# Splitting the closing of a mixer step in a DeltaNet + RWKV-7 decoder block: branch A's norm, gate and store traced behind branch B's projections

## The chip, the cores and the metric

The kernel runs on one core of one Trainium2 chip. The time is device time in microseconds, from one launch to its end. The engines are named as the profile names them: PE is TensorE (PEld its weight loads), DVE is VectorE, ACT is ScalarE, POOL is GpSimd, SP is the sync engine, which here issues most DMAs.

## The reference, cut to what matters

One decoder block in float32 on 1024 tokens of width 1024, with 16 learned tokens ahead of them: half a SwiGLU, then two mixers side by side on the same normed input, merged and projected, then another half SwiGLU.

```python
u = _rmsnorm(h, mix_norm[l])
aq, ak, av, az, abeta, aalpha, bcols, ga, gb = jnp.split(u @ w_in[l], ...)
o_a = _deltanet_branch(aq, ak, av, az, abeta, aalpha, ...)   # A: 8 heads of 128
o_b = _rwkv7_branch(bcols, ...)                              # B: 16 heads of 64
merged = jax.nn.sigmoid(ga) * o_a + jax.nn.sigmoid(gb) * o_b
h = h + merged @ w_out[l]
...
# the end of A (what `finish_a` computes), o from the chunked scan:
o = o * lax.rsqrt(jnp.mean(o * o, axis=-1, keepdims=True) + EPS) * out_gain
o = o.reshape(bsz, t, A_WV) * jax.nn.silu(z)
# the end of B (what stays in `finish`), y from the scan:
y = (y - mean) * lax.rsqrt(var + B_GN_EPS) * ln_gain + ln_bias
y = y + jnp.sum(r * k * r_k, axis=-1, keepdims=True) * v
return y.reshape(bsz, t, B_W) * gate
```

## The kernel before

Activations lie transposed: 128 channels on the partitions, tokens along the free axis. The two SwiGLU halves (`ffn1`, `ffn2`) stand at the two ends; `middle` holds the mixers, from about 700 to 2260 us of the span.

**Steps.** The mixers run in 16 steps: two segments of tokens (528 tokens with the learned ones, then 512), and in each eight groups `j` of 128 channels, one head of A and two heads of B. Steps 0 to 7 are the first segment, 8 to 15 the second. In the text a step n is counted from its `bq` matmuls, the last of its chain (step 10: 1826.0 to 1913.7 us). Each step consists of actions:

- `decay`: B's decay factors (`pw`, `pa` on PE, `sw`, `av` on ACT, the scan `Ls` on DVE).
- `new_b`: B's three projections v, k, r (each `pp`, 24 products of 512 columns in the second segment, 48 of 272 or 256 in the first), the token shift, the key norm (column sum `cs<-hl,bdr`), and the bonus: `bv` is made on DVE, split on ACT and DVE into a high and a low part `hl`, summed over channels on PE (`bon`), and multiplied by v on DVE.
- `new_a`: A's projections k, q, v, its short convolution (`acc` on DVE), SiLU (`xr` on ACT), and the norms of k and q (`cs<-hl,onesr`).
- `operands`, `inverses`: the chunks' triangular matrices and their inversion. `inverses` is 31 pairs `tb`, `Xb` on DVE, each depending on the one before.
- `merge_blocks`, `transitions`, `chains`: the merge of the inverses (`iv`), the transition products (`xp`, `mp`, `np`) and the serial scan over chunks (`p`, `b`, `pq`, closed by `bq`).
- `gates`: three projections (z and the two merge gates) and `gat`.
- `finish`: the closing. For A: squares of the scan's output `oa` (it lies in the tile `kq`), split in two parts `hl`, their sum over channels by two PE products with a matrix of ones (`cs<-hl,onesr`), rsqrt as Ln and Exp (`ro`), two DVE products. For B the same with a block matrix (`cs<-hl,bdr`, `rg`), and four DVE operations on `yb`. Then `yb += oa` and one DMA of `yb` (128x512 float32) to the buffer `mdr`.

**What sets the order.** The program text is traced in the order of strings (`REGULAR` and four others for special steps), where `x+` means action `x` of the next step and `x++` of the step after that. A list scheduler turns this into one fixed order per engine at compile time: among what it takes to be ready it prefers what was traced first. Every engine then executes its own list strictly in that order, and waits on semaphores. DMAs issued by SP stand in one list too.

**Shared tiles.** `ro`, `rg` and one tile of `gates` share one buffer (tag `ro`). The pair `hl` of a column sum is one buffer: its next user waits until the products of the last one are done. `kq`, `Va`, `yb` exist twice, `zg` and `gg` once. A projection's split weights `w` exist twice: ACT makes the high part (line 162), DVE the low part (line 163).

## Time and profile before

| | us |
|---|---|
| time before, median of 3 runs (lowest, highest) | 2966.39 (2959.74, 2974.48) |
| the profiled execution: time, span | 2963.86, 2961.3 |
| PE busy in the span | 2847.0 (96%) |
| DVE busy | 2209.8 (75%) |
| ACT busy | 1445.5 (49%) |
| POOL busy | 522.5 (18%) |
| 40 slices | PE 9 tenths or more in nearly all, PEclk 9 in all |

How to read it: PE bounds the kernel nearly everywhere, so a change can only gain PE's idle time, or time in which PE's clock is not granted in full. The share of a stage is what counts, and in the mixers DVE is nearly as busy as PE. In a timeline row the columns are start in us, length in us, engine, line, operation, out<-in, shapes and count; the bracket at its end is the idle time of the engine ahead of it and what released it. Rows of one line that follow each other are merged.

### The profile page before, as it was taken

The page shows a single profiled execution, that of the slowest core. Times are in us where ns is not written, and L with a number is a line of the kernel's source. Part 1 is how long each engine was busy: PE and PEld are TensorE (multiplying, and loading weights), DVE is VectorE, ACT ScalarE, POOL GpSimd, SP SyncE. Part 2 cuts the span into 40 slices and gives each one's busy share as a digit, 9 for nine tenths or more (in the row PEclk, how much of TensorE's full clock was granted, in tenths as well). Part 3 has the DMA queues.
Part 4 walks back from the last instruction along what each step waited for, and adds up shares of the span by engine and source line. Part 5 has one row for each costly group of instructions (what it writes and reads, how often), then busy time and mean ns, then how long its engine had stood idle before and what let it go on. Part 6 is the DMA issues. An engine that isn't in the chain of part 4 may idle for free. (4 is left out here: it accounts for less than half of the span.)

```text
span 2961.3 us, 60777 instructions
## 1 busy us (share of the span) xinstructions
PE 2847.0 (96%) x24552; PEld 2472.5 (83%) x24552; DVE 2209.8 (75%) x4119; ACT 1445.5 (49%) x2511; POOL 522.5 (18%) x630
## 2 busy tenths in 40 slices
PE   8999999999989999999998999999999999999998
PEld 8999999999878887888776777777777888888887
DVE  8666668776677887788867887778876866667886
ACT  6322234336555656556566556556644432223443
POOL 0332232323000000011001010111101032332521
PEclk9999999999999999999999999999999999999999
DMA  5333236553222322323332332233354332223763
GB/s 213 126 108 108 95 120 215 174 192 125 67 75 75 87 66 73 84 76 86 97 88 74 82 84 72 75 87 83 105 143 175 129 113 102 97 98 129 258 215 109
DMA packets 287897, 339.17 MB, mean 115 GB/s; under 512 B 172704, under 2 KB 181024, under 8 KB 287616
## 3 DMA queue, kind: packets, MB, share of 16 engines
q1 hardware_dynamic: 283600, 326.10, 35.3%
q0 software_dynamic: 2000, 6.56, 0.6%
q8 instruction: 193, 3.16, 0.4%
q10 hardware_dynamic: 2016, 2.63, 0.3%
q14 instruction: 88, 0.72, 0.1%
HBM read 267.57 MB, written 73.41 MB: 115 GB/s over the span
## 5 line engine op out<-in xcount | busy, mean ns | idle before, releaser
L314 PE MATMUL pp<-uk,w 128*128 128x512 f32 (+2 forms) x4824 | 978.6, 348 | 16.8 <-DVE w L163 9.1
L314 PEld LDWEIGHTS pp<-uk,w 128*128 128x128 f32 x4824 | 749.2, 191 | 111.5 <-DVE w L163 12.6
L741 PE MATMUL pd<-form,w 128*128 128x256 f32 (+2 forms) x2904 | 438.0, 313 | 4.7 <-DVE w L163 4.7
L741 PEld LDWEIGHTS pd<-form,w 128*128 128x128 f32 x2904 | 404.3, 190 | 38.1 <-DVE w L163 5.9
L520 PE MATMUL pg<-bt,w 128*128 128x256 f32 (+2 forms) x2520 | 401.6, 318 | 2.5 <-DVE w L163 2.5
L520 PEld LDWEIGHTS pg<-bt,w 128*128 128x128 f32 x2520 | 360.3, 188 | 36.4 <-DVE w L163 3.7
L526 DVE TENSOR_TENSOR c<-c,pg 128x520 f32<-128x520 f32 (+1 forms) x280 | 189.6, 689 | 243.6 <-PE pg L520 220.4
L163 DVE TENSOR_TENSOR w<-wraw,w 128x1024 fp32r<-128x1024 f32 (+1 forms) x254 | 336.5, 1325 | 37.5 <-ACT w L162 36.0
L520 PE MATMUL pg<-b,w 128*128 128x256 f32 (+2 forms) x2160 | 348.1, 317 | 0.0
L162 ACT ACTIVATE w<-wraw 128x1024 fp32r<-128x1024 f32 (+1 forms) x254 | 267.3, 1053 | 160.9 <-PE pg L520 117.1
L520 PEld LDWEIGHTS pg<-b,w 128*128 128x128 f32 x2160 | 309.8, 188 | 28.3 <-DVE w L163 0.2
L162 ACT ACTIVATE w<-wrx 128x1024 fp32r<-128x1024 f32 (+1 forms) x64 | 58.4, 912 | 277.8 <-PE pg L520 241.8
L490 POOL TENSOR_TENSOR wrx<-wrx 128x512 f32<-128x512 f32 x38 | 52.5, 1380 | 611.9 <-DVE w22b L163 352.6
L163 DVE TENSOR_TENSOR form<-form 128x520 fp32r<-128x520 f32 (+1 forms) x152 | 145.3, 991 | 12.4 <-ACT form L162 11.8
L162 ACT ACTIVATE w<-wsum 128x768 fp32r<-128x768 f32 x96 | 75.7, 789 | 158.6 <-PE pd L741 127.2
L163 DVE TENSOR_TENSOR w<-wsum,w 128x768 fp32r<-128x768 f32 x96 | 114.2, 1195 | 37.1 <-ACT w L162 37.0
L241 POOL TENSOR_TENSOR wsum<-wsum,wraw 128x768 f32<-128x768 f32 (+1 forms) x48 | 96.4, 2022 | 205.0 <-DMA wraw<-in_wdn 196.9
L1705 DVE TENSOR_TENSOR Xb<-Xb,tb 115x126 f32<-115x126 f32 (+22 forms) x496 | 125.4, 253 | 8.2
L162 ACT ACTIVATE form<-form 128x520 fp32r<-128x520 f32 (+1 forms) x152 | 93.8, 632 | 76.3 <-DMA form<-frm 72.0
L1703 DVE TENSOR_TENSOR tb<-Ub,Xb 115x126 f32<-115x126 f32 (+22 forms) x496 | 125.1, 252 | 8.0
L1513 DVE SCALAR_TENSOR_TENSOR acc<-xr,pk,acc 128x528 f32<-128x528 f32 (+1 forms) x144 | 109.1, 758 | 24.1 <-ACT acc L1509 23.4
L314 PE MATMUL pwo<-uk,w 128*128 128x512 f32 x384 | 94.7, 397 | 2.7 <-DVE ho L1180 1.5
(445 smaller groups left out, 4360.8 us busy)
## 6 DMA issues: line engine op xcount, KB each, us to landing
wraw<-in_win SPq DMA_DIRECT2D x150, 512.0 KB
wraw<-in_wgu SPq DMA_DIRECT2D x44, 512.0 KB
wrx<-in_wgu SPq DMA_DIRECT2D x44, 512.0 KB
frm<-c SPq DMA_DIRECT2D x76, 260.0 KB
form<-frm SPq DMA_DIRECT2D x76, 260.0 KB
frm<-c SPq DMA_DIRECT2D x76, 256.0 KB
form<-frm SPq DMA_DIRECT2D x76, 256.0 KB
wraw<-in_wdn SPq DMA_DIRECT2D x34, 384.0 KB
```

Of the source, the lines that this page charges most:

```text
L162: g.nc.scalar.activation(hi, src, AF.Copy)
L163: (eng or g.nc.vector).tensor_tensor(lo, src, hi.bitcast(F32), op=ALU.subtract)
L241: g.nc.gpsimd.tensor_tensor(s, x, y, op=ALU.add if r == 1 else ALU.subtract)
L314: g.last_product = g.nc.tensor.matmul(ps, lhsT=l, rhs=r, start=i == 0, stop=i == n - 1)
L490: sums.tensor_tensor(a22, a21, a22, op=ALU.add)
L520: nc.tensor.matmul(ps[:, c0 : c0 + cn], lhsT=l[:, x, k, :], rhs=r[:, k, y, c0 : c0 + cn], start=i == 0, stop=i == 3 * HK - 1)
L526: nc.vector.tensor_tensor(o, x, y, op=ALU.add)
L741: nc.tensor.matmul(pd[:, c0 : c0 + cn], lhsT=wd[:, u, k - k0, :], rhs=x[:, v, c0 : c0 + cn], start=k + i == 0, stop=k == HF - 1 and i == 2)
L1513: nc.vector.scalar_tensor_tensor(acc[:, :n], xr[:, tap : tap + n], V("convw", ct * 4 + tap), acc[:, :n], op0=ALU.mult, op1=ALU.add)
L1703: nc.vector.tensor_tensor(tv, U[:, i, i + 1 :].unsqueeze(2).to_broadcast([npt, nt, ncc]), X[:, i, 0:ncc].unsqueeze(1).to_broadcast([npt, n ...
L1705: nc.vector.tensor_tensor(X[:, i + 1 :, 0:ncc], X[:, i + 1 :, 0:ncc], tv, op=ALU.add)
```

## The change

`finish` is cut in two. B's half keeps the name and the place. A's half, with the sum of both and the store, becomes `finish_a`. In the regular steps and in the switch step it is traced behind `new_b` of two steps ahead and in front of `new_a`; in the three other orders it follows `finish` directly. No operation is added or removed; the only other difference inside a closing is that B's operations now come ahead of A's.

```diff
-REGULAR = "merge_blocks transitions operands+ inverses+ chains gates finish decay++ new_b++ new_a++"
-BEFORE_SWITCH = "... chains gates finish banks gates+ segment decay++ new_b++ tokens++ new_a++"
-SWITCH = "merge_blocks transitions operands+ inverses+ chains finish decay++ new_b++ new_a++"
-LAST_BUT_ONE = "merge_blocks transitions operands+ inverses+ chains gates finish"
-FINAL = "gates merge_blocks transitions chains finish fill"
+REGULAR = "merge_blocks transitions operands+ inverses+ chains gates finish decay++ new_b++ finish_a new_a++"
+BEFORE_SWITCH = "... chains gates finish finish_a banks gates+ segment decay++ new_b++ tokens++ new_a++"
+SWITCH = "merge_blocks transitions operands+ inverses+ chains finish decay++ new_b++ finish_a new_a++"
+LAST_BUT_ONE = "merge_blocks transitions operands+ inverses+ chains gates finish finish_a"
+FINAL = "gates merge_blocks transitions chains finish finish_a fill"
...
 def finish(g, q):
     nc, st, V, j = g.nc, g.st, g.V, q.j
-    oa, yb, zg, gg = q.oa, q.yb, q.zg, q.gg
-    sq = q.Va.rearrange("p c m -> p (c m)")
-    ro = st.tile([P, FULL], F32, name="ro", tag="ro")
-    colsum_rsqrt(g, "ones", oa, sq, ro, FULL, 1.0 / P, V("eps"), pool="ch")
-    nc.vector.tensor_tensor(oa, oa, ro, op=ALU.mult)
-    nc.vector.scalar_tensor_tensor(oa, oa, V("aog"), zg, op0=ALU.mult, op1=ALU.mult)
+    yb = q.yb
     sq = q.AR[:, :NCB].rearrange("p c m -> p (c m)")
     ...
-    nc.vector.tensor_tensor(yb, yb, gg, op=ALU.mult)
+    nc.vector.tensor_tensor(yb, yb, q.gg, op=ALU.mult)
+
+
+def finish_a(g, q):
+    nc, st, V, j = g.nc, g.st, g.V, q.j
+    oa, yb = q.oa, q.yb
+    sq = q.Va.rearrange("p c m -> p (c m)")
+    ro = st.tile([P, FULL], F32, name="ro", tag="ro")
+    colsum_rsqrt(g, "ones", oa, sq, ro, FULL, 1.0 / P, V("eps"), pool="ch")
+    nc.vector.tensor_tensor(oa, oa, ro, op=ALU.mult)
+    nc.vector.scalar_tensor_tensor(oa, oa, V("aog"), q.zg, op0=ALU.mult, op1=ALU.mult)
     nc.vector.tensor_tensor(yb, yb, oa, op=ALU.add)
     if q.it + 1 < 2 * NJ:
         nc.sync.dma_start(g.mdr[q.s][j], yb)
```

What this does to the engines' lists is seen best in step 10. PE behind the chain's last products; before, A's column sum (`cs<-hl,onesr`) stands between the two `pw`:

```order
L1956 MATMUL gat<-gds,ug 128x512 x2
L1956 MATMUL gat<-g_18051,ug 128x512
L1412 MATMUL pw<-ws,upz 128x512
L1292 MATMUL cs<-hl,onesr 128x512 x2
L1413 MATMUL pw<-ws,upz 128x512
L1416 MATMUL pa<-as,upz 128x512
L1417 MATMUL pa<-as,upz 128x512
L314 MATMUL pp<-uk,w 128x512 x5
L1292 MATMUL cs<-hl,bdr 128x512
L314 MATMUL pp<-uk,w 128x512 x2
L1292 MATMUL cs<-hl,bdr 128x512
```

The same place of the same engine in the changed kernel, and then further down, behind the bonus sum `bon`, where A's two products now stand:

```order
L1956 MATMUL gat<-gds,ug 128x512 x3
L1956 MATMUL gat<-g_18051,ug 128x512
L1412 MATMUL pw<-ws,upz 128x512
L1413 MATMUL pw<-ws,upz 128x512
L1416 MATMUL pa<-as,upz 128x512
L1417 MATMUL pa<-as,upz 128x512
L314 MATMUL pp<-uk,w 128x512 x7
L1292 MATMUL cs<-hl,bdr 128x512
L314 MATMUL pp<-uk,w 128x512 x2
L1292 MATMUL cs<-hl,bdr 128x512
L314 MATMUL pp<-uk,w 128x512 x39
```

```order
L314 MATMUL pp<-uk,w 128x512 x37
L1292 MATMUL bon<-hl,bdr 128x512
L314 MATMUL pp<-uk,w 128x512 x7
L1292 MATMUL bon<-hl,bdr 128x512
L314 MATMUL pp<-uk,w 128x512 x4
L1292 MATMUL cs<-hl,onesr 128x512
L314 MATMUL pp<-uk,w 128x512 x2
L1292 MATMUL cs<-hl,onesr 128x512
L314 MATMUL pp<-uk,w 128x512 x22
```

A's sum moved from in front of `new_b`'s 72 products to behind them and `bon`; B's sum now has seven projection products ahead of it instead of five. The list of DVE at the same place, before (`yb<-bq,yb` is the sum that B's closing starts from, `hl<-Va,hl` the low part of A's squares, `hl<-AR,hl` that of B's):

```order
L1307 TENSOR_TENSOR hl<-Va,hl 128x512
L1703 TENSOR_TENSOR tb<-Ub,Xb 115x120
L1705 TENSOR_TENSOR Xb<-Xb,tb 115x20x6
L1927 TENSOR_TENSOR yb<-bq,yb 128x512
L1703 TENSOR_TENSOR tb<-Ub,Xb 115x133
L163 TENSOR_TENSOR w<-wraw,w 128x1024
L1705 TENSOR_TENSOR Xb<-Xb,tb 115x19x7
L1957 TENSOR_TENSOR gg<-gat,gg 128x512
L1703 TENSOR_TENSOR tb<-Ub,Xb 115x126
L1307 TENSOR_TENSOR hl<-AR,hl 128x512
```

And now:

```order
L1703 TENSOR_TENSOR tb<-Ub,Xb 115x133
L163 TENSOR_TENSOR w<-wraw,w 128x1024
L1705 TENSOR_TENSOR Xb<-Xb,tb 115x19x7
L1927 TENSOR_TENSOR yb<-bq,yb 128x512
L1703 TENSOR_TENSOR tb<-Ub,Xb 115x126
L1957 TENSOR_TENSOR gg<-gat,gg 128x512
L1705 TENSOR_TENSOR Xb<-Xb,tb 115x18x7
L163 TENSOR_TENSOR ug<-ugr,ug 128x128
L1703 TENSOR_TENSOR tb<-Ub,Xb 115x136
L1941 TENSOR_TENSOR ug<-ugr,ug 32x128
L1705 TENSOR_TENSOR Xb<-Xb,tb 115x17x8
L1307 TENSOR_TENSOR hl<-AR,hl 128x512
```

A's operation is gone, and `yb<-bq,yb` went from in front of the weight split `w<-wraw,w` to behind it. In the list of DMAs the store `mdr<-yb` moved from ahead of the inverses' traffic to behind it, between two weight loads and the small load `gp`.

## The prediction

> **What bounds the kernel now.** I read the table of engines and the slices first (PE 96% of the span), then the waits of PE in the mixers, then one step in order of time. The windows give the size of what can be won:

> ```profile
> 870.00:2260.00 1390.00, 1321.65 (x14269) 1084.08 (x14267) 1094.74 (x2626) 824.92 (x1579) 118.14 (x309) 0.99 0.31 86
> ...
> 1826.00:1913.70 87.70, 83.05 (x873) 66.36 (x872) 70.51 (x167) 52.50 (x99) 9.22 (x18) 0.98 0.30 81
> 1913.70:1999.80 86.10, 81.45 (x873) 65.12 (x872) 70.44 (x167) 52.54 (x99) 9.23 (x18) 1.00 0.30 83
> ```

> The columns are the stretch, its length, and the busy time of PE, PEld, DVE, ACT and POOL, then the granted clock. From 870 to 2260 us, sixteen steps, PE idles 1390 - 1322 = 68 us. No matmul is added or taken away, so the change can win at most these 68 us, and what a halved clock costs on top. The two step rows are steps 10 and 11: the same work, 1.6 us apart, with a clock of 0.98 and 1.00. Who ends PE's waits in the same stretch:

> ```profile
> PE bon L1292 <- ACT hl L162: 12.2, 13, 1.9
> PE cs L1292 <- ACT hl L1306: 11.8, 19, 1.1
> PE np L1356 <- DVE AR L1842: 9.1, 14, 1.2
> PE pp L314 <- DVE w L163: 5.2, 7, 2.8
> PE cs L1292 <- ACT vka L1805: 5.1, 8, 0.9
> ...
> PE cs L1292 <- DVE yb L1927: 1.5, 1, 1.5
> ```

> Two of these are A's closing itself: `cs` on `vka` and on `yb`, 6.6 us, are A's column sum standing in front of `pw` (row 1829.12 below). The `cs` on `hl` are B's closing and the norms in `new_a`. The first row, the bonus sum, is none of the closing's instructions, but hangs on it, as step 10 shows on PE:

> ```profile
> 1827.86 0.40 PE L1412 MATMUL pw<-ws,upz 128*128 128x512 f32 x1
> 1829.12 0.70 PE L1292 MATMUL cs<-hl,onesr 128*128 128x512 f32 x2 [0.86 <-ACT vka L1805]
> ...
> 1831.50 0.39 PE L1292 MATMUL cs<-hl,bdr 128*128 128x512 f32 x1
> ...
> 1832.18 0.40 PE L1292 MATMUL cs<-hl,bdr 128*128 128x512 f32 x1
> ...
> 1848.46 8.57 PE L314 MATMUL pp<-uk,w 128*128 128x512 f32 x37
> 1858.92 0.50 PE L1292 MATMUL bon<-hl,bdr 128*128 128x512 f32 x1 [1.89 <-ACT hl L162]
> 1859.26 2.84 PE L314 MATMUL pp<-uk,w 128*128 128x512 f32 x7
> ```

> and on DVE, one window and some rows of step 10:

> ```profile
> 1826.90:1861.00 34.10, 31.35 (x176) 24.99 (x169) 33.19 (x77) 22.36 (x39) 7.79 (x14) 0.98 0.41 104
> ...
> 1827.13 0.69 DVE L1307 TENSOR_TENSOR hl<-Va,hl 128x512 fp32r<-128x512 f32 x1
> 1827.74 0.32 DVE L1703 TENSOR_TENSOR tb<-Ub,Xb 115x120 f32<-115x120 f32 x1
> 1828.29 0.69 DVE L1927 TENSOR_TENSOR yb<-bq,yb 128x512 f32<-128x512 f32 x1
> 1829.09 1.22 DVE L163 TENSOR_TENSOR w<-wraw,w 128x1024 fp32r<-128x1024 f32 x1
> 1832.03 0.69 DVE L1967 TENSOR_TENSOR kq<-kq,ro 128x512 f32<-128x512 f32 x1
> 1832.85 0.75 DVE L1968 SCALAR_TENSOR_TENSOR kq<-kq,pk,zg 128x512 f32<-128x512 f32 x1
> 1837.25 0.68 DVE L1975 TENSOR_TENSOR yb<-yb,kq 128x512 f32<-128x512 f32 x1
> 1857.46 0.74 DVE L1485 SCALAR_TENSOR_TENSOR bv<-rB,pk,kB 128x512 f32<-128x512 f32 x1
> ```

> DVE is busy for 33.2 of the 34.1 us from the closing to `bon`. So `bv`, which `bon` waits for, comes when DVE has worked off its list, and every microsecond of A's closing in that list stands ahead of it. That is the main lever of the change, more than A's own wait.

> **The change part by part.** A step's half A is, on PE, two column products; on ACT the square into `Va` (which keeps its place), the square into `hl`, Ln and Exp of `ro`; on DVE the four rows above, `hl<-Va,hl`, two on `kq`, and the last sum on `yb`; on SP one store. All of them move except that one square.

> *A's own wait* goes: the chain's `vka` and the weight split held ACT back from A's `hl`, PE stood 0.86 us. Now `pw` follows `gat` at once. 6.6 us less.

> *B's column sum takes over a part of it.* PE now has twelve products of 0.23 us (8.57 / 37) between the same `gat` and B's first sum (one more `gat`, two `pw`, two `pa`, seven `pp`): 1827.86 + 2.8 = 1830.6. B's `hl` is not there yet. On DVE A's `hl` is gone (-0.61, the distance of the rows 1827.13 and 1827.74), but a `tb`, the weight split and an `Xb` come ahead of `yb` (0.3 + 1.2 + 0.2): it starts at 1829.3 to 1829.4 and ends at 1830.1. ACT needs two squares then:

> ```profile
> 1829.46 0.63 ACT L1305 ACTIVATE AR<-yb 128x512 f32<-128x512 f32 x1
> 1829.98 0.68 ACT L1311 ACTIVATE ro<-cs,pk 128x512 f32<-128x512 f32 x1
> 1830.55 0.63 ACT L1306 ACTIVATE hl<-yb 128x512 fp32r<-128x512 f32 x1
> ```

> They start 0.5 us apart, so `hl` is done at about 1831.3, and PE stands 0.7 us. The low part on DVE has six operations between `yb` and itself, 2.0 us, and ends at 1832.65: PE, two `pp` further, stands another 0.65 us. At 1832.9 it has 39 products ahead of it; before, it had 41 at 1832.4. Nothing is won up to here. In the first segment the same count (12 smaller `pp`, `gat`, `pw`, `pa`, 2.8 us behind the chain, against `hl` some 4 us behind it) gives a wait of about 1.25 us, where now stand 0.5 to 1.1:

> ```profile
> 1080.88 0.50 PE L1292 MATMUL cs<-hl,bdr 128*128 128x512 f32 x1 [0.50 <-ACT hl L1306]
> ...
> 1174.31 0.50 PE L1292 MATMUL cs<-hl,bdr 128*128 128x512 f32 x1 [1.14 <-ACT hl L1306]
> ```

> Costs: 1.4 us in four steps 10 to 13, about 0.5 in steps 8 and 9 each, 0.3 in six steps of the first segment: 5.6 + 1 + 2 = 8.6 us. The bounds are 0 (B's part is ready whenever PE comes) and 19 us (1.5 in each of 13 steps).

> *The bonus sum comes earlier.* Four operations leave DVE's list ahead of `bv`. Each delays the next by 0.60 to 0.66 us, 2.5 us together, and the list stays full: k's and r's projections end where they did, and DVE reaches `kB` and `rB` after them. So `bv` comes at about 1855.0 to 1855.5, ACT's split 0.8 later, and PE comes at 1832.9 + 39, 24 and 37 products + two short groups = 1857.2: no wait left. Of the 12.2 us in the list, the switch step's 1.4 stays (below), and up to 0.8 I leave for small ones: 10 us less. Bounds 4 (only what exceeds a shortening by 0.5) and 12.2.

> *The clock.* Behind the wait of step 10 PE took 2.84 us for seven products, 0.41 instead of 0.23 each:

> ```profile
> 1859.70:1863.10 3.40, 3.40 (x9) 2.64 (x8) 2.26 (x4) 0.00 (x0) 1.71 (x3) 0.50 0.44 155
> 2033.70:2037.10 3.40, 3.40 (x9) 2.67 (x9) 2.49 (x5) 0.00 (x0) 1.52 (x3) 0.51 0.50 161
> ...
> 1946.62 0.50 PE L1292 MATMUL bon<-hl,bdr 128*128 128x512 f32 x1 [1.84 <-ACT hl L162]
> ```

> In steps 10 and 12 the clock was granted by half for one stretch of 3.4 us behind `bon`; in step 11, with a wait of 1.84 us there, it was not, and that step's row above has 1.00. That is the 1.6 us between the steps' lengths. Without the wait the halving goes: 2 x 1.6 = 3.2 us less. [...]

> *The switch step 7* has the largest waits, and no gates' products to fill them:

> ```profile
> 1594.94 0.73 PE L314 MATMUL pp<-uk,w 128*128 128x512 f32 x2 [2.11 <-ACT acc L1509]
> 1597.06 0.80 PE L1292 MATMUL bon<-hl,bdr 128*128 128x512 f32 x1 [1.39 <-ACT hl L162]
> ...
> 1601.72 1.65 PE L314 MATMUL pp<-uk,w 128*128 128x512 f32 x3 [2.85 <-DVE w L163]
> ```

> `bon` comes some 2 us earlier by DVE's list, but PE gets there earlier too (`vp` now stands behind `bon`), and A's two products, which wait for `hl` twice, directly behind. I take 2 us less; bounds +2 and -11 (6.4 of waits and half of the halved clock behind them).

> *A's new place* lies between `bon` and the convolutions of `new_a`. Its cover there, in step 10:

> ```profile
> 1863.00:1885.00 22.00, 20.99 (x255) 15.91 (x256) 14.61 (x26) 19.23 (x36) 0.96 (x4) 1.00 0.19 60
> 1863.81 0.60 ACT L1508 ACTIVATE xr<-pp 128x512 f32<-128x512 f32 x1 [4.93 <-PE pp L314]
> ```

> DVE has 7.4 us free and takes 2.5. ACT has 2.8 free behind 1863 and 4.9 ahead of it: A's `hl` falls into the 4.9, Ln and Exp (1.1 us) into the fuller part. Behind them wait SiLU, a weight split and the first norm's sum of `new_a`, which PE waits for already (0.4 us). I take 1 us over all steps; bounds 0 and 1.1 x 13 = 14. PE's two products there are the ones that left the other place.

> *The store* now stands on SP behind two weight loads and ahead of `gp`. `yb` should be done at about 1866.3, `gp` was issued at 1868.25 and is used on DVE from 1876.5 on, and the loads behind it wait for a weight split anyway:

> ```profile
> 1868.25 0.37 SPq L1570 DMA_DIRECT2D gp<-gdr  x1
> ...
> 1876.52 1.14 DVE L1574 SCALAR_TENSOR_TENSOR E<-gp,tk,ck 128x128 f32<-128x128 f32 x4
> ```

> Nothing, with 8 us of cover. If A came that late, `E` and behind it the chain would wait. The buffers (`ro`, `kq`, `zg`) are taken again only a step or a projection later: nothing.

> Sum: -6.6 + 8.6 - 10 - 3.2 - 2 + 1 = -12.2. The profiled execution took 2963.9 (2961.3 of span and 2.6 around it), which gives 2951.7; it lies 2.5 below the median of the runs, 2966.4, and from that I predict 2954.

> **The rivals.**
> *Nothing takes the wait over.* B's squares are ready when PE comes, since ACT has no `ro` between them, and the switch step runs through. Then the 8.6 fall away, and step 7 gives 6 more: -27, 2939. For it: PE's waits in the first segment are short and the list is the scheduler's own; against it: the weight split ahead of `yb`, which is in the list.
> *Given back on ACT.* The 1.1 us delay `new_a` in all 13 steps, 14 us: +1 or so in all, 2966. For it: ACT is at 19.2 of 22 us there, against it DVE's free time and PE's queue of `pp`.
> *Slower: the halved clock moves to B's sum.* It decides from about 1.86 us of idle within 3.4, as in step 10. If B's wait in the first segment is 2.2 instead of 1.25, six steps pay 1.3 more than now and 1.7 of clock, 18 us, and the other steps only exchange their halving. With `bon` in those six won back (2.7) and the rest of the sum near 0 the time is 2981. Against it: a miss of a microsecond in a list worked out to some tenths. That the change does nothing is excluded by the lists, except in steps 6, 14 and 15.

> **How the numbers follow.** About 0.5%, 15 us, is what a measurement of this kernel can tell from no change. My forecast, 2946 to 2962, gets 0.48, and a third of it is below 2951.6; the first rival 0.22, the second 0.17, the third 0.13. Faster: 0.16 + 0.22 + a little = 0.40; same: 0.32 + 0.17 - 0.02 = 0.47; slower 0.13. The range leaves out the outer ends of the first and third: 2934 to 2974.

> **What would show it.** In the new profile: no wait at A's `cs` of more than some tenths; a wait of 1.0 to 1.5 us at B's (two parts); `bon` almost without one from step 8 on; a clock of 1.00 in steps 9 to 13; step 11 at about 84.5 us instead of 86.1; the waits at `np` as now. The prediction is wrong if DVE idles ahead of `bv` (then the list was not what held it), or if the waits in `new_a` exceed 1 us per step.

## The result, and the profile after

The changed kernel takes 2953.3 us (median of 6 runs, 2942.97 to 2955.89), the kernel before beside it 2964.77. The ratio is 0.9947 with an interval of [0.9931, 0.9963] (the quotient of the two medians is 0.9961); the same kernel run once more in a later set gave 0.9969 [0.9958, 0.9981]. So it is faster, by 0.2 to 0.7% if both intervals are taken together. The prediction was 2954.

The profiled execution took 2947.1 (span 2945.0), 16.7 less than the one of before. Not all of this belongs to the change: the first `bq` came 3.6 us earlier, in a stretch that the change leaves alone (in the later execution of the changed kernel it came 4.9 later). From the first `bq` to that of step 15 are 1348.4 us before, 1334.8 after and 1336.2 in the later execution: 12 to 14 us less, against 12.2 in the sum of the prediction. The windows of the two kernels, steps 0 to 5, 6 to 8 and 9 to 13 (columns as in the prediction):

```profile
896.00:1450.80 554.80, 531.27 (x6253) 454.88 (x6253) 437.51 (x1082) 328.06 (x658) 42.69 (x143) 1.00 0.30 81
1450.80:1739.30 288.50, 268.35 (x2678) 211.25 (x2678) 223.85 (x518) 176.01 (x321) 24.55 (x58) 0.96 0.30 79
1739.30:2173.20 433.90, 412.14 (x4345) 328.74 (x4344) 352.37 (x829) 262.47 (x490) 45.03 (x90) 0.99 0.32 86
```

```profile
892.40:1445.60 553.20, 528.60 (x6246) 453.90 (x6245) 443.73 (x1081) 326.88 (x658) 40.29 (x143) 1.00 0.30 80
1445.60:1731.40 285.80, 268.12 (x2685) 210.49 (x2684) 226.42 (x522) 175.92 (x321) 24.53 (x58) 0.98 0.30 82
1731.40:2155.50 424.10, 411.94 (x4341) 325.51 (x4340) 355.04 (x829) 264.85 (x490) 43.45 (x90) 1.00 0.33 88
```

Steps 9 to 13 give 9.8 us, the three steps around the switch 2.7, steps 0 to 5 of the first segment 1.6. Steps 10 and 11 of the changed kernel are 84.9 and 84.8 us long, both at a clock of 1.00 (87.7 and 86.1 before). The waits of PE in the mixers, from 866.4 to 2242.8 us, which answers to 870 to 2260 before:

```profile
PE np L1356 <- DVE AR L1842: 10.8, 13, 2.6
PE cs L1292 <- ACT hl L1306: 8.8, 18, 1.3
PE bm L1865 <- DVE yb L1848: 5.7, 5, 1.1
PE pw L1412 <- ACT sw L1414: 4.9, 5, 1.0
...
PE pp L314 <- ACT w L162: 4.5, 1, 4.5
PE bon L1292 <- ACT hl L162: 2.3, 7, 1.1
```

`bon` has fallen from 12.2 to 2.3, `cs` on `vka` and on `yb` are gone. Two of the rows shown are new, `bm` on `yb` and `pw` on `sw`, both in the first segment. Step 10 on PE:

```profile
1818.11 0.39 PE L1956 MATMUL gat<-g,ug 128*128 128x512 f32 x1
1818.34 0.39 PE L1412 MATMUL pw<-ws,upz 128*128 128x512 f32 x1
...
1821.60 0.50 PE L1292 MATMUL cs<-hl,bdr 128*128 128x512 f32 x1 [0.57 <-ACT hl L1306]
...
1822.80 0.50 PE L1292 MATMUL cs<-hl,bdr 128*128 128x512 f32 x1 [0.23 <-DVE hl L1307]
1823.14 9.03 PE L314 MATMUL pp<-uk,w 128*128 128x512 f32 x39
...
1838.77 8.57 PE L314 MATMUL pp<-uk,w 128*128 128x512 f32 x37
1847.33 0.50 PE L1292 MATMUL bon<-hl,bdr 128*128 128x512 f32 x1
1847.66 1.79 PE L314 MATMUL pp<-uk,w 128*128 128x512 f32 x7
```

and on DVE and ACT:

```profile
1817.50:1849.50 32.00, 31.20 (x162) 24.50 (x162) 30.72 (x71) 20.70 (x36) 7.29 (x14) 1.00 0.42 101
...
1819.41 0.68 DVE L1927 TENSOR_TENSOR yb<-bq,yb 128x512 f32<-128x512 f32 x1
...
1839.30 0.75 DVE L1206 SCALAR_TENSOR_TENSOR rB<-pp,pk,rB 128x512 f32<-128x512 f32 x1 [0.29 <-ACT rB L1205]
...
1845.86 0.75 DVE L1485 SCALAR_TENSOR_TENSOR bv<-rB,pk,kB 128x512 f32<-128x512 f32 x1
...
1846.64 0.63 ACT L162 ACTIVATE hl<-bv 128x512 fp32r<-128x512 f32 x1
```

The number to read is the distance from `pw` to `bon`: 1858.92 - 1827.86 = 31.06 us before, 1847.33 - 1818.34 = 28.99 after. Of these 2.07 us, 0.23 are `pw`'s own, which now stands behind one more `gat`; counted from the step's first `bq` (1826.0 and 1816.2), `bon` comes at 32.9 and 31.1 us, and the 37 products of r ahead of it begin at 22.5 and 22.6. So nothing is won ahead of r's products, and 1.8 us at `bon`. PE runs through at `bon`, but with nothing to spare: ACT's `hl` ends at 1847.27. DVE, full before, now stands 0.29 us at `rB` because r's projection is not there yet. It has caught up with PE.

### The profile page after: what moved, and what is told of

Read it like the earlier page. It is cut to its first block, busy times and chain, and to the rows that moved or that the text cites. A ratio compares the mean times of both kernels' runs of the same rounds, so it can differ in the third digit from the quotient of the medians.

```text
span 2945.0 us, 60773 instructions
## 1 busy us (share of the span) xinstructions
PE 2843.7 (97%) x24552; PEld 2465.6 (84%) x24552; DVE 2221.7 (75%) x4119; ACT 1445.9 (49%) x2511; POOL 523.0 (18%) x630
## 5 line engine op out<-in xcount | busy, mean ns | idle before, releaser
L314 PE MATMUL pp<-uk,w 128*128 128x512 f32 (+2 forms) x4824 | 974.7, 347 | 15.0 <-ACT w L162 6.5
L314 PEld LDWEIGHTS pp<-uk,w 128*128 128x128 f32 x4824 | 742.6, 191 | 105.6 <-ACT w L162 6.8
L163 DVE TENSOR_TENSOR w<-wraw,w 128x1024 fp32r<-128x1024 f32 (+1 forms) x254 | 335.9, 1323 | 44.7 <-ACT w L162 42.5
L162 ACT ACTIVATE w<-wraw 128x1024 fp32r<-128x1024 f32 (+1 forms) x254 | 267.2, 1052 | 149.8 <-PE pg L520 117.1
L162 ACT ACTIVATE w<-wrx 128x1024 fp32r<-128x1024 f32 (+1 forms) x64 | 58.4, 912 | 278.1 <-PE pg L520 243.0
L163 DVE TENSOR_TENSOR form<-form 128x520 fp32r<-128x520 f32 (+1 forms) x152 | 142.0, 971 | 14.0 <-ACT form L162 13.8
L162 ACT ACTIVATE w<-wsum 128x768 fp32r<-128x768 f32 x96 | 75.7, 789 | 156.3 <-PE pd L741 123.1
L163 DVE TENSOR_TENSOR w<-wsum,w 128x768 fp32r<-128x768 f32 x96 | 118.4, 1238 | 36.3 <-ACT w L162 36.2
L162 ACT ACTIVATE form<-form 128x520 fp32r<-128x520 f32 (+1 forms) x152 | 93.7, 631 | 78.0 <-DMA form<-frm 66.5
L1703 DVE TENSOR_TENSOR tb<-Ub,Xb 115x126 f32<-115x126 f32 (+22 forms) x496 | 124.7, 251 | 8.8
L314 PE MATMUL pwo<-uk,w 128*128 128x512 f32 x384 | 95.2, 398 | 0.9 <-DVE ho L1180 0.9
```

The lines of the kernel that those rows point to most:

```text
L162: g.nc.scalar.activation(hi, src, AF.Copy)
L163: (eng or g.nc.vector).tensor_tensor(lo, src, hi.bitcast(F32), op=ALU.subtract)
L314: g.last_product = g.nc.tensor.matmul(ps, lhsT=l, rhs=r, start=i == 0, stop=i == n - 1)
L1703: nc.vector.tensor_tensor(tv, U[:, i, i + 1 :].unsqueeze(2).to_broadcast([npt, nt, ncc]), X[:, i, 0:ncc].unsqueeze(1).to_broadcast([npt, n ...
```

## The experiments

**Where the gain lies: the move in one segment only.** Both kernels keep the old closing as `finish_ab` in the steps that are not moved.

```diff
-        order = {...}.get(it, REGULAR)
+        order = {..., NJ - 1: PLAIN_SWITCH}.get(it, REGULAR if it >= NJ else PLAIN)   # second_half
+        order = {..., NJ - 1: SWITCH}.get(it, PLAIN if it >= NJ else REGULAR)         # first_half
```

> A's half moved in steps 8 to 13 alone; steps 0 to 7 keep the old closing. Theory (the gain is the shortened DVE list ahead of bv in the second segment): steps 8 to 13 take 505.5 us as in the changed kernel (515.8 before), bon waits for less than 0.2 us there, no stretch of half clock; step 7 stays near 79 us; about 10 us less than before, some 2955. Rival (the gain is spread over the mixers, or is the luck of one profiled execution): 5 us less or fewer, and steps 8 to 13 above 509 us.

Measured: 2952.69 us, ratio 0.9962 [0.9948, 0.9976], 11 us less. Steps 8 to 13 took 506.4 us, `bon` has no wait from step 9 on. The theory holds.

> A's half moved in steps 0 to 5 and in the switch step 7 alone; steps 8 to 13 keep the old closing. Theory: steps 0 to 5 take 553 to 555 us as before and after (waits change places at equal sums), step 7 about 75 us instead of 79, steps 8 to 13 about 516 us with bon waits of 1.5 to 1.9 us; 3 to 5 us less than before, some 2961. Rival (the first segment gains as much as the second): 8 us less or more.

Measured: 2962.5 us, ratio 0.9993 [0.9981, 1.0005], no difference that can be told. Steps 0 to 5 took 553.0 us, step 7 71.3 and step 8 86.5; the border between these two lies elsewhere in this list, so they are read together: steps 6 to 8 took 287.0, 1.5 less than before. Steps 8 to 13 have the waits of the old closing at `bon`, 1.44 to 2.23 us. The two parts add up to what the whole change does.

**Is it the order of the halves, or A's work in the list?**

```diff
-REGULAR = "... gates finish decay++ new_b++ finish_a new_a++"
+REGULAR = "... gates finish finish_a decay++ new_b++ new_a++"
```

`SWITCH` is changed in the same way, here and in the two orders further down.

> The closing is cut and B's half comes first, but A's half follows it directly, ahead of decay++ and new_b++, in every step. Theory (A's DVE operations ahead of bv are the price, not the order of the two halves): they stay ahead of bv, bon still waits 1.5 to 1.9 us in steps 10 to 13, A's wait of 0.86 is exchanged for one of B's of 0.8; within 3 us of before, some 2964. Rival (it is enough that B comes first, because A's sum no longer stands ahead of pw): 8 us less or more, and bon nearly without a wait.

Measured: 2962.98 us, ratio 0.9991 [0.9980, 1.0002], no difference that can be told. `bon` waited 1.09 us in steps 9 to 12, less than I expected. But the distance from `pw` to `bon` says why:

```profile
1830.25 0.39 PE L1412 MATMUL pw<-ws,upz 128*128 128x512 f32 x1
...
1861.38 0.50 PE L1292 MATMUL bon<-hl,bdr 128*128 128x512 f32 x1 [1.09 <-ACT hl L162]
```

31.13 us, as before (31.06). PE only waits elsewhere in between: 0.71 us at B's sum instead of 0.86 at A's, and the rest in pieces too short for the brackets. So B in front wins nothing up to `bon`; A's operations are still ahead of `bv`, and `bon` comes when DVE is through with them. What is gained by the shorter wait at `bon` is that the clock is not halved there in any of the steps 9 to 13, which take 430.6 us instead of 433.9 (mean clock of the profiled execution 0.992, 0.990 before).

**The same list with two operations fewer.**

```diff
-    nc.vector.tensor_tensor(oa, oa, ro, op=ALU.mult)
-    nc.vector.scalar_tensor_tensor(oa, oa, V("aog"), zg, op0=ALU.mult, op1=ALU.mult)
```

> The kernel before without A's two DVE products (rsqrt and gate are computed and not multiplied in): two operations of 0.62 us fewer in DVE's list ahead of bv, PE's order around bon as before. Theory: bon's wait in steps 10 to 13 falls from 1.9 to about 0.6 us, the half clock of steps 10 and 12 is gone, steps 10 to 13 about 84.5 to 85 us; some 8 us less than before. Rival (bv hangs on r's projection and on its own chain of operations, not on the list): the wait of bon stays above 1.5 us.

Measured: 2953.81 us, ratio 0.9964 [0.9950, 0.9977], 11 us less. `bon` waited 1.12, 0.80, 0.86 and 0.42 us in steps 10 to 13 (1.89, 1.84, 1.86, 1.50 before), no clock was halved in steps 9 to 13 (mean clock of the execution 0.993), and the steps took 85.4, 85.1, 85.2 and 84.8 us. PE's order around these rows is that of before, A's wait of 0.87 still there:

```profile
1826.14 0.40 PE L1412 MATMUL pw<-ws,upz 128*128 128x512 f32 x1
1827.40 0.70 PE L1292 MATMUL cs<-hl,onesr 128*128 128x512 f32 x2 [0.87 <-ACT vka L1805]
...
1856.47 0.50 PE L1292 MATMUL bon<-hl,bdr 128*128 128x512 f32 x1 [1.12 <-ACT hl L162]
```

30.33 us from `pw` to `bon` instead of 31.06, 0.73 less here and 1.0 in the other three steps, for two operations of 0.62 us. The rival (above 1.5 us) is out; the wait fell by 0.97 us on average, three quarters of the 1.3 that I expected. A theory that explains `bon` by A's column sum on PE is out as well, since that did not move.

**The same two operations on another engine.** Nothing is left out here; the constant gain `aog` goes into the product that makes `zg`.

```diff
-    nc.vector.tensor_tensor(oa, oa, ro, op=ALU.mult)
-    nc.vector.scalar_tensor_tensor(oa, oa, V("aog"), zg, op0=ALU.mult, op1=ALU.mult)
+    nc.gpsimd.tensor_tensor(oa, oa, ro, op=ALU.mult)
+    nc.gpsimd.tensor_tensor(oa, oa, zg, op=ALU.mult)
```

> The kernel before with A's two products on POOL instead of DVE (the constant gain goes into the gate's product); order of the closing as before, PE's order around bon as before. Theory (the two operations in DVE's list are the price): as without them, bon's wait in steps 10 to 13 falls from 1.9 to 0.8 to 1.1 us, steps 10 to 13 at about 85.2 us, 7 to 11 us less than before. Rival (POOL holds DVE up, as both work on the same memory, or the later yb holds the next step): bon's wait stays above 1.5 us and the time within 4 us of before.

Measured: 2996.59 us, ratio 1.0112 [1.0094, 1.0130], 32 us slower. The theory of the list is not at fault: the list got longer. First POOL, then DVE in step 10:

```profile
1850.85 1.30 POOL L1967 TENSOR_TENSOR kq<-kq,ro 128x512 f32<-128x512 f32 x1 [3.86 <-ACT ro L1313]
1852.23 1.30 POOL L1968 TENSOR_TENSOR kq<-kq,zg 128x512 f32<-128x512 f32 x1
```

```profile
1845.96 0.29 DVE L1705 TENSOR_TENSOR Xb<-Xb,tb 115x126 f32<-115x126 f32 x1
...
1850.91 1.39 DVE L1705 TENSOR_TENSOR Xb<-Xb,tb 115x126 f32<-115x126 f32 x1
1852.33 1.35 DVE L1703 TENSOR_TENSOR tb<-Ub,Xb 115x136 f32<-115x136 f32 x1
1853.72 0.30 DVE L1705 TENSOR_TENSOR Xb<-Xb,tb 115x136 f32<-115x136 f32 x1
```

The same `Xb` of 115x126 takes 0.29 us alone and 1.39 while POOL's product runs, and beside POOL's second product a `tb` takes 1.35; both end 0.15 us behind the product beside them. DVE loses 2.2 us where it should save 1.2, `bon` waits 2.2 us (1.8 in step 13), and the clock is halved behind it in every one of the steps 9 to 13 (mean clock of the execution 0.986). Why the one takes longer beside the other, these rows do not show.

**B's sum: can its wait go too?**

```diff
-REGULAR = "... chains gates finish decay++ new_b++ finish_a new_a++"
+REGULAR = "... chains gates decay++ finish new_b++ finish_a new_a++"
```

> The changed kernel with B's half traced behind decay++ instead of ahead of it (all steps): B's column sum stands behind 23 products of v's projection instead of 7 in steps 8 to 13, and 33 products later in the first segment. Theory: B's wait at cs (0.8 us a step in steps 9 to 13, 1.3 in step 8) is gone; bv was ready with no slack (hl done at 1847.3, bon at 1847.3), so bon takes 0.3 to 0.6 us of it back; steps 9 to 13 at about 84.3 us instead of 84.8; 2 to 5 us less than the changed kernel, some 2949 beside a kernel before of 2965. Rival (PE is not held by bv, the whole 0.8 is won): 83.9 us a step, 6 us less or more. Rival (nothing, since the wait only moves to bon): 84.8 us a step.

Measured: 2959.12 us, ratio 0.9987 [0.9976, 0.9999], so most of the gain is gone; steps 9 to 13 at 85.4 us instead of 84.8. My theory was wrong. PE has 23 products ahead of B's sum now and still waits longer:

```profile
1838.67 0.50 PE L1292 MATMUL cs<-hl,bdr 128*128 128x512 f32 x1 [1.37 <-ACT hl L1306]
```

```profile
1835.70 0.63 ACT L1305 ACTIVATE AR<-yb 128x512 f32<-128x512 f32 x1
1836.95 0.63 ACT L1425 ACTIVATE sw<-Ls 128x512 f32<-128x512 f32 x1 [0.61 <-DVE Ls L1422]
1837.48 0.61 ACT L1428 ACTIVATE ELx<-Ls 128x512 f32<-128x512 f32 x1
1838.00 0.61 ACT L1306 ACTIVATE hl<-yb 128x512 fp32r<-128x512 f32 x1
```

In these lists, what is traced later stands later on every engine that it uses. B's squares went behind the whole of `decay` on ACT, the second of them behind an operation that itself waits for DVE, and that is more than the cover on PE grew by.

> The old closing in steps 0 to 7, and in steps 8 to 13 A's half moved and B's half behind decay++. Theory: the first segment neither gains nor loses by the cut, so this stands within 2 us of the same kernel with the move in all steps; steps 9 to 13 at about 84.3 us. Rival (the new waits of the first segment, pw on sw and bm on yb, 2.1 us a step, are a loss hidden elsewhere): 5 us less than with the move in all steps.

Measured: 2959.02 us, ratio 0.9982 [0.9968, 0.9997]; steps 10 to 13 at 85.5 us, steps 0 to 5 at 557.4 (558.1 in the run above). Its median is within 1 us of that run's, so the first segment makes no difference either way here; the 84.3 us were wrong for the same reason.

**Only the order of one weight split.** The call that hands over v's weights fetches and splits k's on the way; here it is made to follow `yb<-bq`, the sum that B's closing starts from (the lines that pass `w` on are left out).

```diff
+    with ExitStack() as behind:
+        if it >= 2:                      # yb_late: if it >= NJ + 2
+            behind.enter_context(g.tc.issue_after(g.ysum.ins))   # g.ysum: yb<-bq
+        w = loadw(g, "win", 48 + j)      # v's weights; fetches and splits k's on the way
```

> The changed kernel with k's weight split queued on DVE behind yb<-bq, as it stood before. The compiler's list then puts B's first sum behind 2 products instead of 7. Theory of the prediction (the weight split ahead of yb is what makes B's part late): hl comes about 1.2 us earlier, and with the sum where it stood the wait would be gone; here PE comes 1.2 us earlier too, so B's wait stays at 0.5 to 0.9 us and the time within 2 us of the changed kernel. Rival (B's part is late because of ACT, not DVE): the wait grows to 1.8 us or more.

Measured: 2956.72 us, ratio 0.9976 [0.9963, 0.9988]. B's wait in steps 8 to 13 is 0.76 us in one piece, where the changed kernel has 0.57 and 0.23 in two (1.33 in step 8); the steps from 9 on take 84.5 us instead of 84.8. In step 7 the wait at B's sum became 1.89 us. As expected, PE comes earlier by what B's part comes earlier. The same edit in steps 8 to 13 alone, beside the changed kernel itself:

> The changed kernel itself, run beside the two others of this set so that they can be compared on one chip. Expected: ratio to before 0.993 to 0.997 as the first time; steps 9 to 13 at 84.8 us again, the 4.5 us wait for a weight split in step 6 and the 2.6 us wait at np in step 5 again (both are in the lists); if one of the two is gone it was the luck of one execution.

> The changed kernel with k's weight split queued behind yb<-bq in steps 8 to 13 alone, where that gave 84.5 instead of 84.8 us a step; the first segment as in the changed kernel. Theory: 2 us less than the changed kernel in the profile, which the comparison cannot tell from none. Rival (the fewer microseconds of the run with it in all steps were a loss in steps 8 to 13): 84.8 us or more.

Measured: the changed kernel 2954.67 us, ratio 0.9969 [0.9958, 0.9981]; with the edit 2950.35, ratio 0.9955 [0.9941, 0.9969]. Steps 9 to 13 take 84.8 and 84.5 us in the two profiles. It has the lowest median of the study, but its interval overlaps those of the changed kernel, whose first set had the lower ratio (0.9947). The long waits of steps 5 and 6 came again (2.49 and 4.47 us), so they are in the lists.

The 0.3 us a step are seen in the traces alone.

**A's half further back.**

```diff
-REGULAR = "... finish decay++ new_b++ finish_a new_a++"
+REGULAR = "... finish decay++ new_b++ new_a++ finish_a"
```

> A's half traced behind new_a++ instead of behind new_b++. Theory (ahead of new_a++ it costs next to nothing, 0.16 us at the first norm's sum): no gain from moving it further, and the store, gates' buffers and the next chain are nearer; 0 to 4 us more than the changed kernel. Rival (it delays new_a++ by its ACT work, 1 us a step): 8 us less or more.

Measured: 2970.67 us, ratio 1.0022 [1.0009, 1.0035], slower than before. I expected at most 4 us more than the changed kernel. Steps 6 to 13 are not the reason (710.3 us, 710.0 in the changed kernel): the loss is in steps 0 to 5, 569.8 instead of 553.2. Each of them has this wait:

```profile
1229.87 3.35 PE L314 MATMUL pp<-uk,w 128*128 128x512 f32 x7 [1.49 <-DVE w L163]
```

A weight split on DVE now comes late. These waits come to 8.9 us, where the loss is 16.6, and they are not alone: B's sum, which in the changed kernel waits in step 0 only, waits 1.1 to 1.5 us in each of the steps 1 to 5. That A's DVE work ahead of them is the cause fits, but was not tried by itself.

## Why the prediction was right or wrong

The time (2954 against 2953.3) and the sum (-12.2 against -12 to -14 in the mixers) came out, and the main lever was the right one. Not every term was, and some errors cancel. That the medians agree within 0.7 us is luck: the six runs of the changed kernel lie between 2942.97 and 2955.89.

- **A's own wait, -6.6:** right in that it went; the rows are gone, and A's two products run without a wait in steps 8 to 13 (0.72 us in step 7). The reason that I gave for it was misread. A's `hl` was not held back:

```profile
1826.47 0.62 ACT L1306 ACTIVATE hl<-kq 128x512 fp32r<-128x512 f32 x1
...
1828.46 0.58 ACT L1805 ACTIVATE vka<-xp 128x512 f32<-128x512 f32 x1
```

  Its high part was done at 1827.09 and its low part on DVE at 1827.82; the sum started at 1829.12, when `vka` had ended at 1829.04. `vka` empties `xp`, and in the program `xp` and A's `cs` take turns in the same pair of buffers for PE's results (tag `ch`). So the sum waited for its buffer and not for its input.
- **B's sum takes over, +8.6:** right in steps 10 to 13, in the steps and in the size. PE starts its 39 products 1823.14 - 1818.11 = 5.03 us behind the start of the last `gat`; I had 1832.9 - 1827.86 = 5.04. The brackets show 0.57 + 0.23 = 0.8 us and not 1.4, because a bracket counts from the modelled end of the matmul ahead and not from where the next could have begun (the `cs` at 1822.80 is put at 0.50 us, and the product behind it begins 0.34 us after its start); it is the same delay by two measures. My sum mixes them: the 6.6 are brackets, the 8.6 are starts. In starts the two terms cancel, as the text of the prediction has it ("Nothing is won up to here"), and r's products at 22.5 and 22.6 us confirm it. In brackets, the waits at B's sum rose from 0.9 to 5.4 us over steps 8 to 13. (Between `yb` and B's low part DVE's list has seven operations, not six; the time was right.)
- **In the first segment** I had B's wait growing by 0.3. It went away in steps 1 to 5, and `pw` waits there instead:

```profile
1069.59 0.53 PE L314 MATMUL pp<-uk,w 128*128 128x272 f32 x3
1071.11 0.39 PE L1412 MATMUL pw<-ws,upz 128*128 128x272 f32 x1 [0.99 <-ACT sw L1414]
...
1072.84 0.39 PE L1292 MATMUL cs<-hl,bdr 128*128 128x512 f32 x1
```

  `pw` and `pa` stood inside the chain and now stand behind it. I counted them as cover for B's sum and did not ask what the second `pw` waits for: ACT's `sw` of the first. That is 4.9 us in five steps, and with the new wait of `bm` on `yb` (5.7) it is offset by smaller waits elsewhere: PE's idle time in steps 0 to 5 is 23.5 us before and 24.6 after. This step failed in its mechanism and not in its sum.
- **The bonus sum, -10:** right, 9.9 in the brackets, and for the reason given: in the kernel before `bv` hangs on DVE's list (31.06, 31.13, 30.33 and 28.99 us from `pw` to `bon` in four kernels, as A's operations stand ahead of it or not). What I did not see is how close it ends. I had `bv` 2.0 to 2.5 us earlier (1855.0 to 1855.5 instead of 1857.46), and counted from the first `bq` it came 1.8 earlier; `hl` is done 0.06 us before `bon`. I had also written that DVE idling ahead of `bv` would prove me wrong. It idles 0.29 us at `rB`: in the changed kernel the list is no longer what holds `bv`, r's projection is. Two more kernels say the same. With k's weight split later (`yb_late`) and with `decay++` ahead of B's half, PE reaches `bon` of step 10 by 0.3 us earlier and by 0.6 us later than in the changed kernel, and `hl` is done 0.05 and 0.06 us ahead of it again. So a still shorter list could win nothing more at this place.
- **The clock, -3.2:** the halved stretches of steps 10 and 12 are gone, as predicted. The rule that I read from the trace, that 1.86 us of wait halves and 1.84 does not, was wrong. `first_half` has the old closing in steps 8 to 13, and there 2.23 and 1.90 us halved nothing, 2.04 and 1.82 did:

```profile
1689.33 0.50 PE L1294 MATMUL bon<-hl,bdr 128*128 128x512 f32 x1 [2.23 <-ACT hl L162]
...
1775.70 0.50 PE L1294 MATMUL bon<-hl,bdr 128*128 128x512 f32 x1 [2.04 <-ACT hl L162]
```

```profile
1687.71:1691.12 3.41, 1.79 (x8) 1.42 (x8) 3.41 (x6) 1.15 (x2) 3.23 (x5) 1.00 0.75 166
1691.12:1694.54 3.42, 3.42 (x17) 2.77 (x16) 2.58 (x5) 1.88 (x4) 0.76 (x2) 1.00 0.48 153
1773.00:1776.41 3.41, 1.37 (x6) 0.83 (x6) 3.38 (x5) 2.23 (x4) 3.17 (x6) 1.00 1.15 257
1776.41:1779.82 3.41, 3.41 (x10) 2.64 (x9) 2.27 (x4) 0.00 (x0) 1.78 (x3) 0.50 0.53 162
```

  In the traces of the kernels before and after, the changes of the clock stand on a grid of 3.413 us. With `first_half` laid on such a grid, the wait of 2.23 is split over two windows (3.41 - 1.79 = 1.62 us of idle in the second), the wait of 2.04 lies in one (2.04), and the window behind that one is at 0.50. In step 11 of the kernel before, 1.62 of the 1.84 us lay in one window. In these cases the halving went with the place of the wait and not with its length; my reading of the trace was from too few cases.
- **The switch, -2:** 2.7 less over steps 6 to 8 in the first execution, 0.7 in the second. The wait of 2.85 for a weight split in step 7 is gone, but step 6 has one of 4.5 (before: 3.25 at `vbp` and 0.74), and step 5, which I did not look at, one of 2.6 with a halved clock behind it (2.49 and no halved clock in the second execution):

```profile
1412.87 1.13 PE L1356 MATMUL np<-at,BKt 64*64 64x64 f32 x26 [2.62 <-DVE AR L1842]
```

- **A's new place, +1:** right in steps 8 to 13, where the first norm's sum in `new_a` even waits less (0.16 us, 0.41 to 0.45 before). "The waits at `np` as now" was wrong: 0.34 us instead of 0.77 there, about as much as `iv` and `xp` wait longer. Behind `bon`, step 11 takes some 0.5 us more than before, which is about what A's two products take that now stand there.
- **The store:** no cost; `gp` was issued at 1857.8 and `E` started at 1863.9 without a wait.

Of the rivals, "nothing takes the wait over" is out: B's sum waits in each of the steps 8 to 14. The one that ended slower had B's wait grow in the first segment; it did not. "Given back on ACT" would have shown in `new_a` and did not.

## What to carry to other kernels

When a wait names an engine that is busy all the time up to it, ask which operations stand ahead in that engine's list and need not: taking two off it (1.24 us) moved `bon` by 0.7 to 1.0 us, taking four off (2.5 us) by 1.8, while reordering PE around it only moved the place of the wait. A gain of this kind ends where the next producer (here r's projection) takes over, so measure the slack that is left before moving more. Under such a scheduler, a piece that was traced later went later on all engines; more cover on one of them is no gain if its producers fall back on another.

## What the runs showed of the hardware that was not expected

Beside an elementwise product on POOL, 1.30 us long, DVE's `Xb` took 1.39 us instead of 0.29 (`pool_before`).
